# Splitting one weight pair ahead: the order of VectorE's work around the seven-product pairs of a two-layer trunk

## The chip, the cores and the metric

The kernel runs on one core of one Trainium2 chip. The metric is the device time of one execution in microseconds (us). Three executions of the kernel before took 2253.49, 2255.65 and 2257.12 us, median 2255.65 us. A fourth execution was profiled: it took 2254.6 us, and the profile covers 2252.8 us of it.

## The reference

A trunk of two pre-norm residual layers, each a token mixer followed by a SwiGLU feed-forward block (FFN). Layer 0 mixes with HGRN2 and layer 1 with gated linear attention (GLA); both share their input projection with a cross-attention into 256 memory tokens. Sequence 256, model width 2048, FFN width 5632, everything in fp32. Cut to what the change touches:

```python
mem_n = _rmsnorm(mem, norm_mem)
h = x
for layer in range(DEPTH):                      # DEPTH = 2
    hn = _rmsnorm(h, norm_mix[layer])
    if layer % NUM_MIXERS == 0:
        y, xq = _hgrn2_mixer(hn, ...)           # hn @ w_in, then the recurrence
    else:
        y, xq = _gla_mixer(hn, ...)             # the same with q, k, v, g, gk_low, xq
    xa = _memory_attention(xq, mem_n, w_mem_kv[layer])
    h = h + jnp.concatenate([y, xa], axis=-1) @ w_out[layer]
    hn = _rmsnorm(h, norm_ffn[layer])
    gate, up = jnp.split(hn @ w_gate_up[layer], 2, axis=-1)     # 2048 x (2 * 5632)
    h = h + (jax.nn.silu(gate) * up) @ w_down[layer]            # 5632 x 2048
return _rmsnorm(h, norm_final)
```

## The kernel before, in words

**How a product is made.** A product of fp32 matrices is made from halves of each operand: a high part, rounded to the matmul's type, and the low rest. Three matmuls make one product: activations high by weights high, high by low, low by high. The activations' halves are made once per layer; the weights' halves are made as the weights come in.

**How the work is tiled.** Weights arrive as `raw` tiles of 128 partitions by 4 pieces of 512 columns (three buffers). The four pieces are the two row blocks of a *pair* of contraction blocks, crossed with two column blocks c0 and c1. `split` (L276-L303) makes the two halves of a piece or of two pieces: ScalarE writes the high part (a cast) and VectorE subtracts it from the raw piece and writes the low part. The results stand in `parts` tiles (six buffers), or in `part` tiles when only one piece is split (two buffers). The names in the profile carry the number of the raw tile and a letter for the split: `parts128a`, `parts128b`, `parts128c`, `parts128d`. Nearly every instruction is recorded as L151, the wrapper that issues it, so that the tile names tell what an instruction is.

**The kinds of pair.** A 2x2 block product is made plainly with eight products of 128x128 by 512 (24 matmuls), or from seven products of sums and differences (21 matmuls). In the FFN's up part the string `KINDS` gives the kind of each of the eight pairs of an up block: S is a seven-product pair, O a plain one and H a mixed one (both 24 matmuls). All blocks from the fifth on have the plan "SSSSSOSS". There are 11 up blocks of 512 columns per layer, hence seven of these *steady* blocks in each layer, fourteen in all. The pairs of a block are numbered from 0, so that the plain pair is number 5 and the pair ahead of it number 4.

**What a seven-product pair costs VectorE.** `seven` (L451-L466) issues, in this order: the *a* split of raw piece 0; the *b* split of pieces 2 and 3; a subtraction that changes piece 0 (`raw<-raw 128x512`, called *less* here); a subtraction that changes pieces 2 and 3 (`raw<-raw 128x1024`, called *both_less*); the *c* split of pieces 0 and 1; the *d* split of pieces 2 and 3. *less* reads piece 1, to which a second DMA on GpSimd's queue (L444) has added the other row block. *both_less* reads what *less* wrote and writes what *b* reads. *c* reads what *less* wrote, and *d* what *both_less* wrote. A plain pair has two splits of two pieces each; a mixed pair has these, a subtraction, and a split of one piece. In the last pair of a block the summed piece stands in a tile of its own (`T`, `load_apart`), and *c* is split in two instructions.

**What sets the order.** In the FFN each engine executes its instructions in the order of the program (`Engine.kept`). There, TensorE uses the splits of a pair in the order a, b, c, d (products 1, 3, 2, 6, 7, 5, 4; `project_halves`, L627-L668). Between *b* and *less* of each pair a callback `mark` lets work that has come due be issued: copies, gates, transposes and the sums of a finished block (`WHEN`). In the mixer stages a scheduler orders the instructions by its own estimates. The key/query projection of GLA (stages gk0 and gk1, 384 columns, in `gla_pair`) follows a plan in `project_two` (L567-L625) in which "-" is a plain pair.

**The sums.** A finished up block stands in seven PSUM banks. `sums` in `ffn` combines them with seven VectorE additions; two of them release GpSimd to make a low part of the down weights (L300).

## Time and profile before

| what | us |
|---|---|
| median of three executions (lowest, highest) | 2255.65 (2253.49, 2257.12) |
| profiled execution: time, span of its profile | 2254.6, 2252.8 |
| TensorE (PE) busy | 2238.6, 99% of the span |
| VectorE (DVE) busy | 2031.5, 90% |
| ScalarE (ACT) busy | 1452.8, 64% |
| GpSimd (POOL) busy | 280.4, 12% |
| steady blocks of layer 0, 720 to 1168 us: PE busy, DVE busy | 448.0 of 448.0, 426.0 of 448.0 |
| GLA mixer, 1195 to 1480 us: PE busy, DVE busy | 282.4 of 285.0, 224.6 of 285.0 |
| granted TensorE clock | 0.999 of full speed |

A row of the timeline reads: start in us, duration in us, engine, line, operation, tile written, tiles read, shape, how many instructions the row joins, and in brackets the idle time before it and what ended that. The next row of an engine may start before the row ahead of it ends. A row "x2" joins two instructions, and its duration runs from the first one's start to the last one's end. For TensorE the ends are modelled, so that the distance between starts is the safer measure: three matmuls of 512 columns start 0.68 us apart from the next three.

### The profile page before, as it was taken

The page shows a single profiled execution, that of the slowest core. Times are in us where ns is not written, and L with a number is a line of the kernel's source. Part 1 is how long each engine was busy: PE and PEld are TensorE (multiplying, and loading weights), DVE is VectorE, ACT ScalarE, POOL GpSimd, SP SyncE. Part 2 cuts the span into 40 slices and gives each one's busy share as a digit, 9 for nine tenths or more (in the row PEclk, how much of TensorE's full clock was granted, in tenths as well). Part 3 has the DMA queues.
Part 4 walks back from the last instruction along what each step waited for, and adds up shares of the span by engine and source line. Part 5 has one row for each costly group of instructions (what it writes and reads, how often), then busy time and mean ns, then how long its engine had stood idle before and what let it go on. Part 6 is the DMA issues. An engine that isn't in the chain of part 4 may idle for free.

```text
span 2252.8 us, 30400 instructions
## 1 busy us (share of the span) xinstructions
PE 2238.6 (99%) x10668; PEld 1894.6 (84%) x10668; DVE 2031.5 (90%) x2551; ACT 1452.8 (64%) x2010; POOL 280.4 (12%) x275
## 2 busy tenths in 40 slices
PE   9999999999999999999999999999999999999998
PEld 7888888888888888888889999988888888888887
DVE  6879899898998999999996887889999999999997
ACT  7656656565666666666665665566566676666664
POOL 1000100000111112112210000000011221212110
PEclk9999999999999999999999999999999999999999
DMA  8656655656687778878865445566677878887874
GB/s 296 215 168 213 199 182 177 200 193 190 198 236 232 229 234 231 230 230 238 244 221 168 141 156 182 164 209 197 208 221 224 233 230 238 242 238 236 231 233 167
DMA packets 255628, 477.28 MB, mean 212 GB/s; under 512 B 18255, under 2 KB 47731, under 8 KB 255219
## 3 DMA queue, kind: packets, MB, share of 16 engines
q1 hardware_dynamic: 228547, 420.21, 55.5%
q0 software_dynamic: 25632, 50.87, 13.0%
q10 hardware_dynamic: 1296, 4.26, 0.5%
q8 instruction: 84, 1.38, 0.2%
q14 instruction: 69, 0.57, 0.1%
HBM read 472.12 MB, written 3.15 MB: 211 GB/s over the span
## 4 chain that ended last, share of the span: by engine, by line
PE 90%; DVE 6%; issue 2%; DMA 1%; ACT 1%; SPq 0%; POOL 0%; DVEq 0%; POOLq 0%; ACTq 0%
PE f_p L151 34%; PE fd L151 18%; PE wo L151 4%; PE m1p L151 2%; PE hv2p L151 2%; PE hv1p L151 2%; PE hf0p L151 2%; PE hv0p L151 2%; PE wo1p L151 2%; PE hf2p L151 2%; PE hf1p L151 2%; PE wo0p L151 2%; PE m0p L151 2%; PE gk0p L151 1%; PE gk1p L151 1%
## 5 line engine op out<-in xcount | busy, mean ns | idle before, releaser
L151 DVE TENSOR_TENSOR raw<-raw 128x1024 f32<-128x1024 f32 (+3 forms) x330 | 311.2, 943 | 16.7 <-DMA raw<-in_w_down_dram 5.6
L151 ACT CAST parts<-raw 128x1024 fp32r<-128x1024 f32 (+1 forms) x216 | 211.7, 1016 | 56.8 <-DMA raw<-in_w_down_dram 14.7
L151 DVE TENSOR_TENSOR parts<-raw,parts 128x1024 fp32r<-128x1024 f32 (+1 forms) x176 | 200.2, 1171 | 22.7 <-ACT parts L151 22.0
L444 POOL DMA_DIRECT2D raw<-in_w_gate_up_dram x92 | 80.4, 873 | 541.2 <-DMA raw<-in_w_gate_up_dram 274.7
L300 POOL TENSOR_TENSOR parts<-raw,parts 128x1024 fp32r<-128x1024 f32 x40 | 95.6, 2406 | 113.5 <-ACT parts L151 81.2
L151 ACT COPY h<-fd 128x512 f32<-128x512 f32 x80 | 45.7, 588 | 46.5 <-PE fd L151 44.0
L428 POOL DMA_DIRECT2D T<-in_w_gate_up_dram x36 | 21.1, 587 | 430.2 <-DVE hf_4g L151 82.7
L151 ACT ACTIVATE s<-s,rf_r 128x512 f32<-128x512 f32 x44 | 31.8, 723 | 42.0 <-DVE s L151 42.0
L151 DVE SCALAR_TENSOR_TENSOR s<-e,rf_r,s 128x512 f32<-128x512 f32 x44 | 45.7, 1076 | 2.9 <-ACT s L151 0.5
L151 DVE TENSOR_TENSOR e<-f_p,e 128x512 f32<-128x512 f32 x66 | 45.2, 684 | 2.6 <-DVE s L151 0.5
L429 POOL DMA_DIRECT2D T<-in_w_gate_up_dram x36 | 31.0, 861 | 120.4 <-DMA T<-in_w_gate_up_dram 111.1
L151 ACT COPY fd<-h 128x512 f32<-128x512 f32 x82 | 45.2, 582 | 0.0
L444 POOL DMA_DIRECT2D raw<-in_hgrn_w_in_dram x17 | 14.7, 867 | 209.9 <-DMA raw<-in_hgrn_w_in_dram 124.6
L151 PE MATMUL fd<-parts,s_0h 128*128 128x512 f32 x128 | 39.8, 392 | 0.0
L151 PE MATMUL fd<-parts,s_4h 128*128 128x512 f32 x128 | 39.8, 392 | 0.0
L151 PE MATMUL fd<-parts,s_8h 128*128 128x512 f32 x128 | 39.8, 392 | 0.0
L151 PE MATMUL fd<-parts,s_2h 128*128 128x512 f32 x128 | 39.8, 392 | 0.0
L151 PE MATMUL fd<-parts,s_6h 128*128 128x512 f32 x128 | 39.8, 392 | 0.0
L151 PE MATMUL fd<-parts,s_1h 128*128 128x512 f32 x128 | 39.4, 389 | 0.0
L151 PE MATMUL fd<-parts,s_3h 128*128 128x512 f32 x128 | 39.4, 389 | 0.0
L151 PE MATMUL fd<-parts,s_5h 128*128 128x512 f32 x128 | 39.4, 389 | 0.0
L151 PE MATMUL fd<-parts,s_7h 128*128 128x512 f32 x128 | 39.4, 389 | 0.0
(6020 smaller groups left out, 7434.0 us busy)
## 6 DMA issues: line engine op xcount, KB each, us to landing
raw<-in_w_gate_up_dram SPq DMA_DIRECT2D x224, 512.0 KB, 4.4
raw<-in_w_down_dram SPq DMA_DIRECT2D x80, 1024.0 KB, 5.5
raw<-in_w_gate_up_dram SPq DMA_DIRECT2D x220, 256.0 KB, 4.2
raw<-in_hgrn_w_in_dram SPq DMA_DIRECT2D x79, 512.0 KB, 4.6
raw<-in_gla_w_in_dram SPq DMA_DIRECT2D x96, 384.0 KB, 3.3
raw<-in_w_gate_up_dram POOLq DMA_DIRECT2D x92, 256.0 KB, 4.9
T<-in_w_gate_up_dram POOLq DMA_DIRECT2D x72, 256.0 KB, 5.0
raw<-in_w_out_dram SPq DMA_DIRECT2D x16, 1024.0 KB, 5.1
```

The source lines that it names most:

```text
L151: ins = func(*args, **kwargs)
L300: low = (nc.gpsimd if free_port else ve).tensor_tensor(out=both[:, 1, k:j, 0:m], in0=src[:, k:j, :], in1=both[:, 0, k:j, 0:m].bitcast(F32) ...
L428: nc.gpsimd.dma_start(out=both[:, 0, :], in_=rows[0])
L429: nc.gpsimd.dma_start(out=both[:, 0, :], in_=rows[1], accum_op=ALU.add)
L444: nc.gpsimd.dma_start(out=raw[:, 1, 0:n], in_=rows[1], accum_op=ALU.add)
```

## The change

Four edits, none of which changes what is computed.

1. In `project_halves` and `project_two` the raw tile of the next pair is taken, and its *a* split is issued, inside the present seven-product pair between *c* and *d* (argument `ahead`). In `project_two` this is done only where both pairs are seven-product pairs. In a mixed pair the next pair's *a* split is issued ahead of its last split.
2. In a pair that was begun so, *less* is issued ahead of *b*. In a pair with its sum in a tile of its own, *both_less* is issued between the two halves of *c*.
3. `sums` makes its seven additions in another order; the releases stand at the first and the fourth.
4. The plans of gk0 and gk1 become "-----SS-" where they were "------S-": one more seven-product pair in each.

In the FFN the change moves VectorE's instructions as follows. The rows are those of pair 4 and the plain pair 5 of the fifth block of layer 0, on VectorE; `raw_6235` is the raw tile of pair 4 and `raw_6278` that of pair 5. Before:

```order
L151 TENSOR_TENSOR parts128a<-raw_6235,parts128a 128x512
L151 TENSOR_TENSOR parts128b<-raw_6235,parts128b 128x1024
L151 TENSOR_TENSOR raw_6235<-raw_6235 128x512
L151 TENSOR_TENSOR raw_6235<-raw_6235 128x1024
L151 SCALAR_TENSOR_TENSOR parts128c<-raw_6235,parts128c 128x1024
L151 TENSOR_TENSOR parts128d<-raw_6235,parts128d 128x1024
L151 TENSOR_TENSOR parts129a<-raw_6278,parts129a 128x1024
L151 TENSOR_TENSOR parts129b<-raw_6278,parts129b 128x1024
```

The same place with the change, where the tile numbers are `raw_6171` for pair 3, `raw_6211` for pair 4 and `raw_6254` for pair 5:

```order
L151 TENSOR_TENSOR parts128a<-raw_6211,parts128a 128x512
L151 TENSOR_TENSOR parts127d<-raw_6171,parts127d 128x1024
L151 TENSOR_TENSOR raw_6211<-raw_6211 128x512
L151 TENSOR_TENSOR parts128b<-raw_6211,parts128b 128x1024
L151 TENSOR_TENSOR raw_6211<-raw_6211 128x1024
L151 SCALAR_TENSOR_TENSOR parts128c<-raw_6211,parts128c 128x1024
L151 TENSOR_TENSOR parts129a<-raw_6254,parts129a 128x1024
L151 TENSOR_TENSOR parts128d<-raw_6211,parts128d 128x1024
L151 TENSOR_TENSOR parts129b<-raw_6254,parts129b 128x1024
```

Each *a* has moved ahead of the *d* of the pair before, and *less* ahead of *b*. The *a* of a plain pair is two pieces wide (1024 columns), that of a seven-product pair one (512). TensorE's order of use is unchanged in the FFN.

In the GLA stage gk0 the scheduler gives another order too. The rows are VectorE's towards the end of the stage; `gsq` and `gsk` are the sums of the stage's products from PSUM (`gk0p`), `Tg` are decay products, and 232, 233 are raw tiles of the stage that follows. Before:

```order
L151 TENSOR_TENSOR Tg_10701<-GF_10518 128x512
L151 TENSOR_TENSOR Tg_10701<-Tg_10701 128x256
L151 TENSOR_TENSOR parts231b<-raw_10626,parts231b 128x2x384
L151 TENSOR_TENSOR gsq_10637<-gk0p_10605,gsk_10635 128x2x192
L151 TENSOR_TENSOR parts232a<-raw_10676,parts232a 128x2x384
L151 TENSOR_TENSOR gsk_10635<-gk0p_10609,gsq_10637 128x2x192
L151 TENSOR_TENSOR parts232b<-raw_10676,parts232b 128x2x384
L151 TENSOR_TENSOR gsq_10637<-gk0p_10613,gsk_10635 128x2x192
L151 TENSOR_TENSOR gsq_10637<-gk0p_10613,gsq_10637 128x2x192
L151 TENSOR_TENSOR Tg_10701<-Tg_10701 128x128
L151 TENSOR_TENSOR parts233a<-raw_10752,parts233a 128x2x384
L151 TENSOR_TENSOR gsk_10635<-gk0p_10276,gsk_10635 128x2x192
```

With the change:

```order
L151 TENSOR_TENSOR parts231b<-raw_10632,parts231b 128x2x384
L151 TENSOR_TENSOR gsq_10643<-gk0p_10584,gsk_10641 128x2x192
L151 TENSOR_TENSOR parts232a<-raw_10682,parts232a 128x2x384
L151 TENSOR_TENSOR gsk_10641<-gk0p_10588,gsq_10643 128x2x192
L151 TENSOR_TENSOR parts232b<-raw_10682,parts232b 128x2x384
L151 TENSOR_TENSOR gsq_10643<-gk0p_10592,gsk_10641 128x2x192
L151 TENSOR_TENSOR gsq_10643<-gk0p_10592,gsq_10643 128x2x192
L151 TENSOR_TENSOR gsk_10641<-gk0p_10276,gsk_10641 128x2x192
L151 TENSOR_TENSOR gsk_10641<-gk0p_10280,gsk_10641 128x2x192
L151 TENSOR_TENSOR gsq_10643<-gk0p_10288,gsq_10643 128x2x192
L151 TENSOR_TENSOR gsq_10643<-gk0p_10284,gsq_10643 128x2x192
L151 TENSOR_TENSOR Tg_10707<-GF_10518 128x512
```

All sums now stand ahead of the first `Tg`; before, three `Tg` and the split 233a stood ahead of the first of the closing `gsk` sums.

The diff:

```diff
-    def split(src, name, by=2, turned=False):
+    def split(src, name, by=2, turned=False, between=None):
         if isinstance(src, list):
             ...
             for k in (1, 0):
                 ...
+                if k:
+                    between()
...
-    def seven(i, raw, fed, between=None):
+    def seven(i, raw, fed, between=None, b00=None, ahead=None):
         n = raw.shape[2]
         tt = ve.tensor_tensor
-        b00, = split(raw[:, 0:1, :], f"{i}a")
+        apart = fed if fed and fed is not True else None
+        begun = b00 is not None
+
+        def less():
+            tt(out=raw[:, 0, :], in0=apart[:, 0, :] if apart else raw[:, 1, :], in1=raw[:, 0, :], op=ALU.subtract)
+
+        def both_less():
+            tt(out=raw[:, 2:4, :], in0=raw[:, 2:4, :], in1=raw[:, 0:1, :].broadcast_to([P, 2, n]), op=ALU.subtract)
+
+        if not begun:
+            b00, = split(raw[:, 0:1, :], f"{i}a")
+        if not fed:
+            tt(out=raw[:, 1, :], in0=raw[:, 1, :], in1=raw[:, 2, :], op=ALU.add)
+        if fed and begun:
+            less()
         b11, b10 = split(raw[:, 2:4, :], f"{i}b")
         if between:
             between()
-
-        if not fed:
-            tt(out=raw[:, 1, :], in0=raw[:, 1, :], in1=raw[:, 2, :], op=ALU.add)
-        apart = fed if fed and fed is not True else None
-        tt(out=raw[:, 0, :], in0=apart[:, 0, :] if apart else raw[:, 1, :], in1=raw[:, 0, :], op=ALU.subtract)
-        tt(out=raw[:, 2:4, :], in0=raw[:, 2:4, :], in1=raw[:, 0:1, :].broadcast_to([P, 2, n]), op=ALU.subtract)
-        t6, t7 = split([raw[:, 0:1, :], apart] if apart else raw[:, 0:2, :], f"{i}c", turned=True)
+        if not (fed and begun):
+            less()
+        if apart:
+            t6, t7 = split([raw[:, 0:1, :], apart], f"{i}c", turned=True, between=both_less)
+        else:
+            both_less()
+            t6, t7 = split(raw[:, 0:2, :], f"{i}c", turned=True)
+        if ahead:
+            ahead()
         t5, t4 = split(raw[:, 2:4, :], f"{i}d")
...
     # project_two
+        def ahead(at):
+            i, raw = come(at)
+            came.append((i, raw, split(raw[:, 0:1, 0:n], f"{i}a")[0]))
+
+        for at, (p, kind) in enumerate(zip(order, plan)):
+            i, raw, b00 = came.pop() if came else (*come(at), None)
             if kind == "S":
-                todo = held(behind, seven, i, raw[:, :, 0:n], fed) if behind else seven(i, raw[:, :, 0:n], fed)
+                more = (lambda: ahead(at + 1)) if plan[at + 1:at + 2] == "S" else None
+                args = seven, i, raw[:, :, 0:n], fed, None, b00, more
...
     # project_halves
+        def ahead(p):
+            if p < len(PAIRS):
+                i, raw = come(p)
+                came.append((i, raw, split(raw[:, 0:1 if kinds[p] == "S" else 2, :], f"{i}a")))
+
+        for p, kind in enumerate(kinds):
+            Engine.kept = keep <= p
+            i, raw, begun = came.pop() if came else (*come(p), None)
             x = forms[p].get
             last = p == len(PAIRS) - 1
             if kind == "S":
-                todo = seven(i, raw, fed, lambda: mark(key + p))
+                todo = seven(i, raw, apart.get(p, True), lambda: mark(key + p), begun and begun[0], lambda: ahead(p + 1))
                 ...
             else:
-                b00, b01 = split(raw[:, 0:2, :], f"{i}a")
+                b00, b01 = begun or split(raw[:, 0:2, :], f"{i}a")
                 ...
                     ve.tensor_tensor(out=raw[:, 3, :], in0=raw[:, 3, :], in1=raw[:, 2, :], op=ALU.subtract)
+                    ahead(p + 1)
                     e1, = split(raw[:, 3:4, :], f"{i}c")
...
     # gla_pair
-        project_two(hq["pairs"], ("------S-", "------S-")[pr], w, kw + pr * 2 * DK, pr * 2 * DK, 2 * DK, f"gk{pr}", give,
+        project_two(hq["pairs"], "-----SS-", w, kw + pr * 2 * DK, pr * 2 * DK, 2 * DK, f"gk{pr}", give,
...
     # sums, in ffn
-                for out, p, q in ((s0, 2, e0), (e1, 6, e0), (s1, 7, e1), (e1, 5, e1), (e0, 5, s1),
+                for out, p, q in ((e1, 6, e0), (s0, 2, e0), (s1, 7, e1), (e0, 5, s1), (e1, 5, e1),
                                   (s1, 4, s1), (e1, 3, e1)):
                     ve.tensor_tensor(out=out, in0=ps[p], in1=q, op=ALU.add)
-                    if p in (2, 5) and out is not e0 and b:
+                    if (p == 6 or out is e0) and b:
                         free_port.append(ve.last)
```

`come` holds the lines that took a raw tile and loaded it; it is called one pair earlier where `ahead` is.

More of the change, by code (lines that the diff above doesn't have):

```diff
@@ L591, in early, with come @@
                 out[:] = onto
-        for at, (p, kind) in enumerate(zip(order, plan)):
+        came = []
+        def come(at):
             i, raw = new_raw()
             if i == 0:
-                load_pair(raw, w, p, c0, c1, n, kind, fed)
+                load_pair(raw, w, order[at], c0, c1, n, plan[at], fed)
             if prep:
@@ L599, in project_two @@
             if i > 0:
-                load_pair(raw, w, p, c0, c1, n, kind, fed)
+                load_pair(raw, w, order[at], c0, c1, n, plan[at], fed)
+            return i, raw
+        def ahead(at):
[3 more added lines that the diff above has]
+            i, raw, b00 = came.pop() if came else (*come(at), None)
             if kind == "S":
-                todo = held(behind, seven, i, raw[:, :, 0:n], fed) if behind else seven(i, raw[:, :, 0:n], fed)
+                more = (lambda: ahead(at + 1)) if plan[at + 1:at + 2] == "S" else None
+                args = seven, i, raw[:, :, 0:n], fed, None, b00, more
+                todo = held(behind, *args) if behind else args[0](*args[1:])
                 last = at == plan.rindex("S")
@@ L638, in product, with come @@
             pe.matmul(ps[b], xl, hi, start=False, stop=left[b] == 0)
-        for p, kind in enumerate(kinds):
-            Engine.kept = keep <= p
+        came = []
+        def come(p):
             i, raw = new_raw()
@@ L644, in project_halves @@
                 apart[7] = load_apart(w, 7, c1)
-            fed = apart.get(p, True)
-            load_pair(raw, w, p, c0, c1, 512, kind, fed)
+            load_pair(raw, w, p, c0, c1, 512, kinds[p], apart.get(p, True))
+            return i, raw
+        def ahead(p):
[5 more added lines that the diff above has]
+            i, raw, begun = came.pop() if came else (*come(p), None)
             x = forms[p].get
```

## The prediction

> **What bounds the kernel now.** I read the page first: busy shares and the chain of waits (shares by engine), then the windows by stage (busy time of PE, PEld, DVE, ACT and POOL, clock, DMA share).
>
> ```profile
> PE 2238.6 (99%) x10668; PEld 1894.6 (84%) x10668; DVE 2031.5 (90%) x2551; ACT 1452.8 (64%) x2010; POOL 280.4 (12%) x275
> PE 90%; DVE 6%; issue 2%; DMA 1%; ACT 1%; SPq 0%; POOL 0%; DVEq 0%; POOLq 0%; ACTq 0%
> 720.00:1168.00 448.00, 448.00 (x2009) 371.37 (x2008) 426.04 (x464) 301.73 (x385) 83.21 (x76) 1.00 0.79 230
> ```
>
> TensorE bounds the kernel, and in the steady blocks nothing interrupts it. VectorE time saved there is worth nothing by itself; VectorE can only lose, by handing a split over later than TensorE comes to it. So I read who arrives first at each split. VectorE's timeline for the fifth block of layer 0:
>
> ```profile
> 731.50 1.23 DVE L151 SCALAR_TENSOR_TENSOR parts125c<-raw,parts125c 128x1024 fp32r<-128x1024 f32 x1 [0.97 <-ACT parts125c L151]
> 732.64 1.22 DVE L151 TENSOR_TENSOR parts125d<-raw,parts125d 128x1024 fp32r<-128x1024 f32 x1
> 733.78 0.68 DVE L151 TENSOR_TENSOR parts126a<-raw,parts126a 128x512 fp32r<-128x512 f32 x1
> 734.38 1.22 DVE L151 TENSOR_TENSOR parts126b<-raw,parts126b 128x1024 fp32r<-128x1024 f32 x1
> 735.51 1.94 DVE L151 TENSOR_TENSOR raw<-raw 128x512 f32<-128x512 f32 x2
> 737.46 1.23 DVE L151 SCALAR_TENSOR_TENSOR parts126c<-raw,parts126c 128x1024 fp32r<-128x1024 f32 x1
> 738.65 1.23 DVE L151 TENSOR_TENSOR parts126d<-raw,parts126d 128x1024 fp32r<-128x1024 f32 x1
> 739.79 0.68 DVE L151 TENSOR_TENSOR parts127a<-raw,parts127a 128x512 fp32r<-128x512 f32 x1
> ...
> 749.51 1.23 DVE L151 SCALAR_TENSOR_TENSOR parts128c<-raw,parts128c 128x1024 fp32r<-128x1024 f32 x1
> 750.70 1.23 DVE L151 TENSOR_TENSOR parts128d<-raw,parts128d 128x1024 fp32r<-128x1024 f32 x1
> 751.84 1.22 DVE L151 TENSOR_TENSOR parts129a<-raw,parts129a 128x1024 fp32r<-128x1024 f32 x1
> ```
>
> VectorE has no idle time after 731.50. A pair takes it 738.65 − 732.64 = 6.01 us, TensorE's 21 matmuls only 21 × 0.227 = 4.76. So its lead shrinks through the S pairs, and the last splits ahead of plain pair 129 arrive just in time. TensorE's timeline there:
>
> ```profile
> 750.74 0.63 PE L151 MATMUL f_p<-parts128c,hf_4h 128*128 128x512 f32 x2
> ...
> 752.14 0.62 PE L151 MATMUL f_p<-parts128d,hf_4h 128*128 128x512 f32 x2
> 752.60 0.40 PE L151 MATMUL f_p<-parts128d,hf_4l 128*128 128x512 f32 x1
> 752.83 0.62 PE L151 MATMUL f_p<-parts128d,hf_4h 128*128 128x512 f32 x2
> ```
>
> 128c's low part ends at 750.74, when TensorE starts on it; 128d's ends at 751.93, 0.21 before its first matmul. The last steady block of layer 1 shows the same (2164.38 − 2164.17 = 0.21), and the two sets of rows stand for all fourteen:
>
> ```profile
> 2162.94 1.23 DVE L151 TENSOR_TENSOR parts404d<-raw,parts404d 128x1024 fp32r<-128x1024 f32 x1
> 2164.38 0.62 PE L151 MATMUL f_p<-parts404d,hf_4h 128*128 128x512 f32 x2
> ```
>
> **How late is too late.** Three places show it, from VectorE's and TensorE's timelines in blocks 0 and 1:
>
> ```profile
> 534.38 1.22 DVE L151 SCALAR_TENSOR_TENSOR parts87c<-raw,parts87c 128x1024 fp32r<-128x1024 f32 x1
> 535.72 1.22 DVE L151 TENSOR_TENSOR parts87d<-raw,parts87d 128x1024 fp32r<-128x1024 f32 x1
> 582.99 1.22 DVE L151 SCALAR_TENSOR_TENSOR parts96c<-raw,parts96c 128x1024 fp32r<-128x1024 f32 x1
> ```
>
> ```profile
> 535.42 0.73 PE L151 MATMUL f_p<-parts87c,hf_3h 128*128 128x512 f32 x2
> ...
> 536.91 0.63 PE L151 MATMUL f_p<-parts87d,hf_3h 128*128 128x512 f32 x2
> ...
> 583.51 0.40 PE L151 MATMUL f_p<-parts96c,hf_4h 128*128 128x512 f32 x1
> 584.26 0.50 PE L151 MATMUL f_p<-parts96c,hf_4h 128*128 128x512 f32 x1 [0.35 <-DVE parts96c L151]
> 584.60 0.39 PE L151 MATMUL f_p<-parts96c,hf_4l 128*128 128x512 f32 x1
> ```
>
> The first matmul of a split needs only the high part, so the low part may end some 0.17 us after it starts: 87d ends 0.03 after and costs nothing; 87c ends 0.18 after and its two matmuls take 0.73 instead of 0.62; 96c ends 0.70 after, and the next start comes 0.75 instead of 0.23 later (0.52 lost) and the one behind it 0.34 instead of 0.23 (0.11 more). So a stall is lateness less 0.17, plus 0.11 for starting again.
>
> **What pins VectorE.** ScalarE's timeline ahead of 731.50:
>
> ```profile
> 729.24 1.27 ACT L151 COPY h<-fd 128x512 f32<-128x512 f32 x2 [2.31 <-PE fd L151]
> 730.40 1.06 ACT L151 ACTIVATE parts125c<-raw 128x1024 fp32r<-128x1024 f32 x1
> ```
>
> VectorE waits 0.97 for 125c's cast, which stands behind copies that wait for TensorE. The copies come due behind *b* of pair 1 before and after the change, so *c* of pair 1 stays at 731.50 on TensorE's clock, and whatever is saved ahead of it is lost in this wait.
>
> **Part 1 and 2, steady blocks.** From the rows: an instruction of two pieces starts its successor after 1.14 when the successor doesn't need it (732.64 to 733.78), one of one piece after 0.60 (733.78 to 734.38). Where each needs the one before, *less* and *both_less* take 1.95 (735.51 to 737.46) instead of 0.60 + 1.14 = 1.74, and *c* to *d* takes 1.19 instead of 1.14; the dependences cost 0.26 per pair. In the new order *both_less* still stands right behind *b*, whose source it overwrites: one wait remains, which I put at about 0.12, half of the 0.21 lost around *both_less*. So the pair comes to 1.14 + 0.60 + 1.14 + 0.60 + 1.14 + 0.12 + 1.14 = 5.88, and from the pinned *c* of pair 1 to *c* of pair 4 it takes 17.64 instead of 749.51 − 731.50 = 18.01. So 128c starts at 749.14, 0.37 earlier, for which TensorE isn't waiting.
>
> Then comes the cost. Between 128c and 128d stands 129a now, and this is of two pieces: 1.14. So 128d starts at 749.14 + 1.14 + 1.14 = 751.42 and ends at 752.65, 0.51 after TensorE's 752.14. Less 0.17 that is 0.34 of stall, and 0.11 to start again: **0.45 per steady block, 6.3 for fourteen**. If the remaining wait were nothing, 128d would end 0.36 earlier, 0.15 after TensorE's start, and the stall would vanish (0 in all); if nothing were saved, 128d would end at 753.06, stall 0.76 + 0.11, 12.2 in all. I stay near the rows. 129a loses nothing, since TensorE reaches it at the end of 128d. In the S pairs that follow VectorE has 3.2 us in hand (plain pair: 2 × 1.14 = 2.28 against 24 × 0.227 = 5.44), so their later *d* and earlier *c* cost and gain nothing.
>
> **Blocks 0 to 3.** In the mixed pairs the next *a* fills the gap ahead of the last split (0.69 idle at such a place), but 96d then takes the delay that 96c loses: about even, from −0.6 to +0.6 per layer. 87d ends 0.03 after its matmul now and gets 88a ahead of it (1.14), of which earlier gains give back perhaps 0.8: +0.3. 106d, ahead of plain pair 107, has 0.37 in hand:
>
> ```profile
> 636.52 1.23 DVE L151 TENSOR_TENSOR parts106d<-raw,parts106d 128x1024 fp32r<-128x1024 f32 x1
> 638.12 0.62 PE L151 MATMUL f_p<-parts106d,hf_4h 128*128 128x512 f32 x2
> 624.87 0.86 POOL L444 DMA_DIRECT2D raw<-in_w_gate_up_dram  x1 [5.58 <-DVE parts104c L151]
> ```
>
> It loses 1.14 and gains perhaps 0.5: +0.2. But *less* now wants the adding DMA that GpSimd issues at 624.87 about 2 us sooner (1.14 for *b*, the rest from the filled gaps), and *b*, which needs none of it, queues behind: up to +0.4 more. Together +0.6 per layer, **+1.2**.
>
> **Part 3** saves two dependences per block, off the path: VectorE has its lead then, and is pinned afterwards. Nothing; were it exposed, 0.2 × 22 = 4 at most.
>
> **Part 4.** Each stage drops three matmuls of 384 columns; twelve start 1245.93 − 1243.85 = 2.08 apart, 0.173 each. That is 0.52 a stage, **−1.0**. VectorE gets about 2.6 us more work, ScalarE 1.2, estimated from the pieces; TensorE leads there are over 0.9 us. The sums move ahead of the decays, so TensorE's wait for ScalarE's scaled keys shrinks:
>
> ```profile
> 1243.85 2.24 PE L151 MATMUL gk0p<-parts226a,hm_3x 128*128 128x384 f32 x12
> 1245.93 1.03 PE L151 MATMUL ap<-ident,prob 128*128 128x128 f32 x8
> ...
> 1278.31 0.44 PE L151 MATMUL tgk<-ident,gsk 128*128 128x128 f32 x2 [0.59 <-ACT gsk L151]
> 1279.56 0.44 PE L151 MATMUL tgk<-ident,gsk 128*128 128x128 f32 x2 [0.80 <-ACT gsk L151]
> ```
>
> Of 1.4, I take **−0.6**; the ends are −1.4 and, if the added work makes a split late, +2.
>
> **Sum** against the profiled execution's 2254.6: +6.3 + 1.2 − 1.0 − 0.6 = +5.9, thus 2260.5. The profiled execution lies 1.0 under the median, and on its scale I predict **2261**.
>
> **A rule against the saving.** The rows above overlap (733.78 starts before 732.64 + 1.22) where there is no dependence, and don't at 737.46. The Trainium skill ("VectorE: DVE Perf Modes", section "The DRAIN you can't avoid") says that the next operation doesn't start before the pipe is empty and that "the semaphore costs nothing extra here"; the same section allows an earlier start to an operation that isn't held. By the first rule reordering would save VectorE nothing; the trace, with 1.95 against 1.74, disagrees.
>
> **Rivals.** (a) *The delay of 128d is covered*: VectorE gains more per pair than I count, or a late low part is tolerated longer. For it: the remaining wait is not in this trace. Against: 96c's stall begins by the same rule. It decides if 128d ends before 752.31, which asks 0.34 more gain over three pairs than the 0.37 counted: nearly the whole of the remaining wait. Then parts 3 and 4 and recovered stalls remain: −1.0 − 0.6 − 1.2, about 2253: not slower. Chance 0.22.
> (b) *The order saves nothing*: what an instruction takes doesn't depend on its neighbour, and 128d is late by all of 1.14 − 0.21 − 0.17, plus 0.11: 14 × 0.87 + 1.2 − 1.6 = +11.8, 2267. For it: *c* to *d* takes 1.19 though they don't depend on each other directly; against: 1.95 against 1.74. Chance 0.08. It is what the skill's rule above would make of this change.
> (c) *`less` at the head of the queue waits for DMA* in steady blocks too: VectorE stands, with *b* and all behind it. From a landing 0.3 us after *less* is wanted, 128d is 0.3 later still: 14 × 0.3 = 4.2 more, 2265. For it: the adding DMA is asked for earlier in every S pair; against: DMA share 0.79, with landings some 5 us after issue. Chance 0.10.
>
> **How the numbers follow.** My forecast has the remaining 0.60, itself spread from 2257 to 2264. Slower by over 0.2% (4.5 us, about what a measurement of this kernel can tell from no change) begins at 2260.2: 0.6 of the forecast, and (b) and (c): 0.54. Faster, under 2251.1, needs (a) with more than its sum: 0.09. The rest, 0.37, is no change. Eight times in ten: 2252.5 to 2266.
>
> **What would show it.** Right: TensorE's second start on 128d's successors in each steady block late by 0.2 to 0.5, put down to VectorE, with 129a just ahead of it; VectorE's pair period near 5.9; *c* of pair 1 still waiting on ScalarE; gk stages 0.5 shorter. Wrong: no wait of TensorE in steady blocks (a); a period of 6.0 (b); VectorE idle ahead of `raw<-raw` for a DMA (c).

## The result

The changed kernel is slower: 2270.39 us in the median of six executions (2269.58 to 2272.92) beside 2254.80 of the kernel before in the same rounds (2252.85 to 2257.12). The ratio is 1.0070, with a 95% interval of 1.0057 to 1.0083: 15.6 us more. The prediction of 2261 had the sign, and its range ended at 2266.

The page of the changed kernel, busy shares and chain of waits by engine:

```profile
PE 2246.2 (99%) x10662; PEld 1892.7 (83%) x10662; DVE 2027.7 (89%) x2561; ACT 1453.7 (64%) x2014; POOL 283.2 (12%) x275
PE 73%; DVE 14%; issue 8%; DMA 2%; ACT 2%; SPq 0%; POOL 0%; ACTq 0%; DVEq 0%; POOLq 0%
```

VectorE does about as much work as before, but its share of the chain that sets the end has gone from 6 to 14%, and TensorE's from 90 to 73%: the chain now leaves TensorE where it waits for a split.

Where the time went is seen best by setting the two traces beside each other at the same place of TensorE's program. In this table the time is that of the first matmul on the split named, after minus before (in the last row the end of the span); the last column is what was added since the row above.

| first matmul on | what lies since the row above | shift, us | added, us |
|---|---|---|---|
| 87d | start, HGRN mixer, up to pair 3 of block 0 | +0.81 | +0.81 |
| 88a | d of pair 3 of block 0 | +1.45 | +0.64 |
| 97a | block 1 | +1.53 | +0.08 |
| 107a | block 2 | +2.83 | +1.30 |
| 117a | block 3 | +4.13 | +1.30 |
| 201a | the seven steady blocks of layer 0 | +7.08 | +2.95 |
| 210d | the down tail of layer 0 | +8.59 | +1.51 |
| 291d | GLA mixer, output projection | +7.47 | −1.12 |
| 292a | block 0 of layer 1 | +8.11 | +0.64 |
| 301a | block 1 | +10.16 | +2.05 |
| 311a | block 2 | +11.24 | +1.08 |
| 321a | block 3 | +12.54 | +1.30 |
| 405a | the seven steady blocks of layer 1 | +15.57 | +3.03 |
| end | the rest | +15.77 | +0.20 |

The fourteen steady blocks add 6.0 and blocks 0 to 3 of both layers 8.4, where 6.3 and 1.2 had been forecast. A steady block of the change, VectorE's timeline and then TensorE's:

```profile
735.64 1.23 DVE L151 SCALAR_TENSOR_TENSOR parts125c<-raw,parts125c 128x1024 fp32r<-128x1024 f32 x1 [1.21 <-ACT parts125c L151]
...
747.39 1.22 DVE L151 SCALAR_TENSOR_TENSOR parts127c<-raw,parts127c 128x1024 fp32r<-128x1024 f32 x1
748.53 0.68 DVE L151 TENSOR_TENSOR parts128a<-raw,parts128a 128x512 fp32r<-128x512 f32 x1
749.13 1.22 DVE L151 TENSOR_TENSOR parts127d<-raw,parts127d 128x1024 fp32r<-128x1024 f32 x1
750.26 0.69 DVE L151 TENSOR_TENSOR raw<-raw 128x512 f32<-128x512 f32 x1
750.87 1.22 DVE L151 TENSOR_TENSOR parts128b<-raw,parts128b 128x1024 fp32r<-128x1024 f32 x1
752.12 1.23 DVE L151 TENSOR_TENSOR raw<-raw 128x1024 f32<-128x1024 f32 x1
753.26 1.22 DVE L151 SCALAR_TENSOR_TENSOR parts128c<-raw,parts128c 128x1024 fp32r<-128x1024 f32 x1
754.39 1.22 DVE L151 TENSOR_TENSOR parts129a<-raw,parts129a 128x1024 fp32r<-128x1024 f32 x1
755.53 1.22 DVE L151 TENSOR_TENSOR parts128d<-raw,parts128d 128x1024 fp32r<-128x1024 f32 x1
```

```profile
756.25 0.39 PE L151 MATMUL f_p<-parts128d,hf_4h 128*128 128x512 f32 x1
756.80 0.50 PE L151 MATMUL f_p<-parts128d,hf_4h 128*128 128x512 f32 x1 [0.17 <-DVE parts128d L151]
757.14 0.40 PE L151 MATMUL f_p<-parts128d,hf_4l 128*128 128x512 f32 x1
```

Pair 1's *c* still waits for ScalarE. A pair now takes VectorE 753.26 − 747.39 = 5.87 us. But 129a stands between 128c and 128d, and 128d ends at 756.75, 0.50 after its first matmul. The next start comes 0.55 later instead of 0.23, and the one behind it 0.34 instead of 0.23. All fourteen blocks show it, with 0.33 of stall in thirteen and 0.61 in one, each with the 0.11 behind it.

In blocks 1 to 3 the same stall is larger and something stands ahead of it. Block 3 of layer 0, VectorE, ScalarE, TensorE:

```profile
682.71 1.22 DVE L151 SCALAR_TENSOR_TENSOR parts115c<-raw,parts115c 128x1024 fp32r<-128x1024 f32 x1
685.61 0.69 DVE L151 TENSOR_TENSOR parts116a<-raw,parts116a 128x512 fp32r<-128x512 f32 x1 [1.68 <-ACT parts116a L151]
686.56 1.23 DVE L151 TENSOR_TENSOR parts115d<-raw,parts115d 128x1024 fp32r<-128x1024 f32 x1 [0.26 <-ACT parts115d L151]
```

```profile
684.95 0.62 ACT L151 CAST parts116a<-raw 128x512 fp32r<-128x512 f32 x1 [3.33 <-PE f_p L151]
685.48 1.05 ACT L151 CAST parts115d<-raw 128x1024 fp32r<-128x1024 f32 x1
```

```profile
693.26 0.39 PE L151 MATMUL f_p<-parts116d,hf_4h 128*128 128x512 f32 x1
694.24 0.50 PE L151 MATMUL f_p<-parts116d,hf_4h 128*128 128x512 f32 x1 [0.60 <-DVE parts116d L151]
```

ScalarE can't cast 116a until TensorE has gone on, and now 115d's cast, which used to stand ahead of it, stands behind it. VectorE waits 1.68 us. 116d used to be ready 0.88 us ahead of its first matmul; now it ends 0.93 behind it (694.19 against 693.26).

Two waits for a DMA stand ahead of *less* with *b* behind them; VectorE in the down tail of layer 0 and in block 1 of layer 1, then TensorE in the tail:

```profile
1165.88 0.69 DVE L151 TENSOR_TENSOR raw<-raw 128x512 f32<-128x512 f32 x1 [5.44 <-DMA raw<-in_w_down_dram]
...
1632.28 0.69 DVE L151 TENSOR_TENSOR raw<-raw 128x512 f32<-128x512 f32 x1 [1.48 <-DMA raw<-in_w_gate_up_dram]
```

```profile
1179.59 1.45 PE L151 MATMUL fd_0p<-parts210c,s_20m 128*128 128x512 f32 x5 [1.30 <-DVE parts210c L151]
```

In the order of before, the tail's wait was 4.01 us long and *b* stood ahead of it; now *b* stands behind.

The down tail of layer 1 has the same order. VectorE there, with the change:

```profile
2216.33 0.69 DVE L151 TENSOR_TENSOR raw<-raw 128x512 f32<-128x512 f32 x1 [4.53 <-DMA raw<-in_w_down_dram]
2216.94 1.22 DVE L151 TENSOR_TENSOR parts413b<-raw,parts413b 128x1024 fp32r<-128x1024 f32 x1
```

Before, 413b stood ahead of the wait, and the wait was 1.60 us. TensorE loses 0.2 at most by it in this execution, but more in several of the runs below.

### The profile page after: what moved, and what is told of

Same layout as the page of the kernel before. It is cut to its first block, busy times and chain, and to the rows that moved or that the text cites. A ratio compares the mean times of both kernels' runs of the same rounds, so it can differ in the third digit from the quotient of the medians.

```text
span 2268.6 us, 30382 instructions
## 1 busy us (share of the span) xinstructions
PE 2246.2 (99%) x10662; PEld 1892.7 (83%) x10662; DVE 2027.7 (89%) x2561; ACT 1453.7 (64%) x2014; POOL 283.2 (12%) x275
## 4 chain that ended last, share of the span: by engine, by line
PE 73%; DVE 14%; issue 8%; DMA 2%; ACT 2%; SPq 0%; POOL 0%; ACTq 0%; DVEq 0%; POOLq 0%
PE f_p L151 19%; PE fd L151 16%; PE wo L151 4%; DVE raw L151 2%; PE m1p L151 2%; PE hv2p L151 2%; PE hv1p L151 2%; PE hv0p L151 2%; PE hf0p L151 2%; PE wo1p L151 2%; PE hf2p L151 2%; PE hf1p L151 2%; PE wo0p L151 2%; PE m0p L151 2%; DMA raw<-in_w_gate_up_dram 2%
## 5 line engine op out<-in xcount | busy, mean ns | idle before, releaser
L151 ACT CAST parts<-raw 128x1024 fp32r<-128x1024 f32 (+1 forms) x216 | 211.7, 1016 | 57.9 <-DMA raw<-in_w_down_dram 15.6
L151 DVE SCALAR_TENSOR_TENSOR s<-e,rf_r,s 128x512 f32<-128x512 f32 x44 | 54.8, 1284 | 2.5
```

The lines of the kernel that those rows point to most:

```text
L151: ins = func(*args, **kwargs)
```

## The experiments

Three theories, each with its place. **T1**: a split of two pieces ahead of *d* makes *d* late (steady blocks, 87d, 291d, and part of blocks 1 to 3). **T2**: a one-piece split taken ahead waits for one of its two buffers, with *d* behind it (blocks 1 to 3). **T3**: *less*, ahead of *b*, waits for its DMA. The rivals of each theory are the other two, or a cause that none of them names. The kernel before was run beside each set: 2255.82 (25 executions) for the first four runs, 2255.03 (19) for the next four, 2255.72 (26) for the last three.

**1. The two-piece split behind d.**

```diff
-        if ahead:
+        if ahead and not late:                 # late: the next pair is plain or mixed
             ahead()
         t5, t4 = split(raw[:, 2:4, :], f"{i}d")
+        if ahead and late:
+            ahead()
```

> The changed kernel with one thing undone: where the next pair is plain or mixed, its two-piece a split is issued behind the d split of the present seven-product pair again, instead of ahead of it. Theory T1 (the wide split ahead of d makes d late): the 14 stalls of 0.45 us at the d of pair 4 of the steady blocks vanish (-6.4), those at 87d and 291d too (-1.3), and the stalls of 0.9 at the d ahead of the plain pair in blocks 1 to 3 (six places, -5.3): about 13 us less than the change, 2 to 3 us over the kernel before. Rival T2 (blocks 1 to 3 lose their time because the a split of pair 4 waits for a buffer): the six places keep most of their 1.25 us each, and the run comes out some 7 to 8 us under the change, 7 to 8 over the kernel before.

2257.04 us (10 executions), ratio to before 1.0007, interval 0.9998 to 1.0017. The fourteen stalls are gone, as are those at 87d and 291d and at the six places of blocks 1 to 3; the whole loss but about 1 us came with this one split's place. VectorE and TensorE in the same block:

```profile
750.84 1.23 DVE L151 TENSOR_TENSOR parts128d<-raw,parts128d 128x1024 fp32r<-128x1024 f32 x1
751.98 1.22 DVE L151 TENSOR_TENSOR parts129a<-raw,parts129a 128x1024 fp32r<-128x1024 f32 x1
```

```profile
752.54 0.61 PE L151 MATMUL f_p<-parts128d,hf_4h 128*128 128x512 f32 x2
```

128d ends 0.47 ahead of its matmul, where before it was 0.21: the 0.26 that reordering saves VectorE by then is real, and TensorE doesn't get it. What stayed were short stalls at 106c, 116c and 320c (0.37, 0.39, 0.39), which T1 doesn't explain, 1.2 in the down tail of layer 0 and 0.8 at 414c in that of layer 1.

With the two-piece split out of the way, the run also shows what the rest of the new order does ahead of plain pair 107. VectorE and TensorE at 106d:

```profile
636.81 1.23 DVE L151 TENSOR_TENSOR parts106d<-raw,parts106d 128x1024 fp32r<-128x1024 f32 x1
```

```profile
638.14 0.61 PE L151 MATMUL f_p<-parts106d,hf_4h 128*128 128x512 f32 x2
```

106d ends only 0.1 ahead of its first matmul, where it was 0.37 before; 116d and 320d are at 0.13 where they were at 0.88.

**2. The buffer's turn.**

```diff
                     ve.tensor_tensor(out=raw[:, 3, :], in0=raw[:, 3, :], in1=raw[:, 2, :], op=ALU.subtract)
+                    mine = single(f"{i}c")     # the one-piece buffer, taken before the next pair's
                     ahead(p + 1)
-                    e1, = split(raw[:, 3:4, :], f"{i}c")
+                    e1, = split(raw[:, 3:4, :], f"{i}c", both=mine)
```

> The changed kernel with one thing undone: in a mixed pair the buffer of its own last split (one piece, one of two buffers) is taken ahead of that of the next pair's a split, as it was before; the order of the instructions stays that of the change. T2: the a split of pair 4 in blocks 1 to 3 (96a, 106a, 116a and the same in layer 1) waits for the buffer of the mixed pair's split, which TensorE has left by then, and no longer for that of the pair just ahead; VectorE no longer stands 1.7 us at 116a; the six places lose 1.25 us each now and 0 to 0.5 then: 4 to 6 us less than the change. T1 alone: the steady blocks keep 0.45 each, and if the wide split is what makes the six places late, they keep 0.9 each: 1.5 to 2.5 us less than the change.

2270.75 us (4 executions), ratio 1.0064, interval 1.0047 to 1.0081: nothing gained. T2 in this form fell. ScalarE waits as long as in the change; its row of this run, and then that of the kernel before:

```profile
686.18 0.62 ACT L151 CAST parts116a<-raw 128x512 fp32r<-128x512 f32 x1 [3.32 <-PE f_p L151]
```

```profile
682.10 0.62 ACT L151 CAST parts116a<-raw 128x512 fp32r<-128x512 f32 x1 [0.84 <-PE f_p L151]
```

With TensorE's shift at the first matmul on 115a or 116c taken off (4.09 here, 2.86 in the change), the cast begins at 682.09 in both, and at 682.10 in the kernel before. The wait was there before too, and which buffer is taken first doesn't move the moment at which it ends.

**3. Both.**

> The changed kernel with both: the wide a split behind d, and the mixed pair's buffer taken first. T1 and T2 together: no stall at any d or c of pair 4; what is left is the stall of 1.5 us in the down tail of layer 0 and whatever less, ahead of b, waits for its DMA (1.5 us of VectorE's time at 300b), against 1 us gained in the two key/query stages: within 2 us of the kernel before, 13 to 15 us under the change. If a third cause of several us is at work, it stays 4 us or more above the kernel before.

2258.57 us (10 executions), ratio 1.0007, interval 0.9998 to 1.0017: the same as the first run within the interval. So the second edit adds nothing to the first either, and no further cause of several us is left. The profiled execution has the stalls of the first run, with 1.75 and 0.9 in the two tails, and one of 0.7 at 404c.

**4. Less behind b as well.**

```diff
-        if fed and begun:
-            less()
         b11, b10 = split(raw[:, 2:4, :], f"{i}b")
...
-        if not (fed and begun):
-            less()
+        less()
```

> As the run with both undone, and in addition less stands behind b again in every begun pair, also in the mixer and tail stages (what remains is one a split ahead of d where both pairs are seven-product pairs, the split c of the last pair, the sums and the key/query plans). T3 (less ahead of b waits for its adding DMA, with b queued behind): the stall of 1.5 us in the down tail goes, as does VectorE's wait ahead of 300b: 1.5 to 2.5 us under the run with both undone. Rival (the dependences it removed were worth something): VectorE's pair grows from 5.87 to some 6.0 us, 128d ends 0.3 later than with both undone, still ahead of TensorE by 0.3: no difference, or up to 2 us more.

2258.61 us (10 executions), ratio 1.0016, interval 1.0006 to 1.0025; the one without is within it. In the trace TensorE's wait at 210c, 1.6 with both undone, is gone, but the edit isn't the reason: *b* still stands behind the wait. 209 is not begun ahead, as a plain pair stands in front of it, so every version of the program has its *b* ahead of *less*; it is the scheduler that turned the two round in the tail. VectorE:

```profile
1159.96 0.69 DVE L151 TENSOR_TENSOR raw<-raw 128x512 f32<-128x512 f32 x1 [3.23 <-DMA raw<-in_w_down_dram]
1160.57 1.22 DVE L151 TENSOR_TENSOR parts209b<-raw,parts209b 128x1024 fp32r<-128x1024 f32 x1
```

The data came earlier this time: with TensorE's shift at 208a taken off, *less* began at 1157.46, against 1159.06 with both undone. So this run doesn't test T3 in the tail, and neither do runs 8 and 9, whose tails have this order as well. Which part of the change made the scheduler choose it, no run shows.

What speaks for T3 there is the set of traces, on the same scale. With *b* behind, 210c stalls by 0.7 to 1.8 us in the four in which *less* began at 1157.9 or later (the change, runs 1, 3 and 5), and at most 0.2 is lost in the five in which it began by 1157.5 (runs 2, 4, 6, 8, 9); run 7 has another order there. With *b* ahead it doesn't stall even at 1158.95 (before) and 1158.76 (run 11). So the order costs up to 1.8 us there when the DMA is late, and nothing when it is early. In the tail of layer 1 the edit leaves the order too, and TensorE loses 0.5 at 414c.

In the FFN, where the edit does take effect, the time didn't get better: against run 3 the steady blocks of layer 0 add about 1 us, in steps of 0.1 to 0.25.

**5. Mixed pairs not ahead.**

```diff
                     ve.tensor_tensor(out=raw[:, 3, :], in0=raw[:, 3, :], in1=raw[:, 2, :], op=ALU.subtract)
-                    ahead(p + 1)
                     e1, = split(raw[:, 3:4, :], f"{i}c")
```

> The changed kernel with one thing undone: a mixed pair no longer splits the next pair's a ahead of its own last split (seven-product pairs still do, two pieces ahead of d included). In the run with the buffer taken first the wait only moved: there 105a, issued ahead of the mixed pair's split 104c, waited for TensorE to leave 103c's buffer. T2, mended (with two buffers and a split more in flight, one of 104c, 105a, 106a waits for TensorE with others behind it): now order and turns are those of before, VectorE no longer stands 2.3 us at 104c or 1.7 at 116a, and of the 7.1 us that blocks 1 to 3 lose in both layers about 2.7 remain (96d 0.8, 106d 0.56, 116d 0, in each layer, by the two-piece split alone): 4 to 5 us under the change, some 11 over the kernel before. Rival (the two-piece split alone makes these places late): 0 to 1 us under the change.

2274.49 us (4 executions), ratio 1.0087, interval 1.0072 to 1.0102: 4 us *worse* than the change, against an expected gain of 4 to 5. Both the expectation and its rival (a gain of 0 to 1) missed. Taking the next split ahead in a mixed pair fills a gap and is a gain: without it block 0 loses 1.09 instead of 0.64, and 95c and 299c stall too. And 116a still waits for TensorE, with 115d behind it:

```profile
687.19 0.62 ACT L151 CAST parts116a<-raw 128x512 fp32r<-128x512 f32 x1 [1.40 <-PE f_p L151]
687.71 1.05 ACT L151 CAST parts115d<-raw 128x1024 fp32r<-128x1024 f32 x1
```

The wait is shorter because ScalarE comes to it later, not because it ends sooner (687.19 − 5.09 of shift = 682.10). So the moment is TensorE's, and what can be chosen is only what stands behind the wait.

**6. Half a dose.** The two-piece split of a plain or mixed pair in two instructions, one ahead of *d*, one behind.

```diff
+                if kinds[p] != "S" and apiece:
+                    halves, piece = by_piece(raw[:, 0:2, :], f"{i}a")
+                    came.append((i, raw, halves))
+                    piece(0)
+                    return lambda: piece(1)    # called behind d
```

> The changed kernel with a dose: the a split of a plain or mixed pair is made piece by piece, the first piece ahead of d and the second behind it. By the rule of the prediction 128d ends 0.54 earlier than in the change, at 752.11 on the time scale of before, 0.03 ahead of its first matmul: no stall in the steady blocks (-6.4), and -0.5 at each of the eight other places: 2259 to 2261. Rival (any split between c and d breaks the handing over, whatever its length): the steady blocks keep their 0.45, 2270.

2260.28 us (10 executions), ratio 1.0023, interval 1.0014 to 1.0032. The steady blocks have no stall. VectorE, TensorE:

```profile
752.99 0.68 DVE L151 TENSOR_TENSOR parts129a<-raw,parts129a 128x512 fp32r<-128x512 f32 x1
753.60 1.22 DVE L151 TENSOR_TENSOR parts128d<-raw,parts128d 128x1024 fp32r<-128x1024 f32 x1
```

```profile
754.85 0.62 PE L151 MATMUL f_p<-parts128d,hf_4h 128*128 128x512 f32 x2
```

128d ends at 754.82, 0.03 ahead, the number expected. What is left over before lies in blocks 1 to 3 (0.2 to 0.4 at each *c* and *d* of pair 4), in the tail of layer 1 (1.1 at 414c), and in parts that the change doesn't touch.

**7. A double dose.** The plain pair's *b* ahead of *d* too.

```diff
                 came.append((i, raw, split(raw[:, 0:1 if kinds[p] == "S" else 2, :], f"{i}a")))
+                if kinds[p] == "O" and kinds[p - 1] == "S":
+                    later_b.append(split(raw[:, 2:4, :], f"{i}b"))
```

> The changed kernel with a double dose: where a plain pair follows, its b split (two pieces) stands ahead of d as well. By the rule 128d ends 1.14 later than in the change: the stall grows from 0.33 + 0.11 to 1.47 + 0.11 in each of the fourteen steady blocks (+16), and by 1.14 at eight other places (those two ahead of a mixed pair keep theirs) (+9): 2294 to 2297. Rival (VectorE has slack that the pin hides): less than half of it, under 2283.

2294.11 us (4 executions), ratio 1.0174, interval 1.0157 to 1.0191: inside the range expected. TensorE:

```profile
759.70 0.39 PE L151 MATMUL f_p<-parts128d,hf_4h 128*128 128x512 f32 x1
761.39 0.50 PE L151 MATMUL f_p<-parts128d,hf_4h 128*128 128x512 f32 x1 [1.30 <-DVE parts128d L151]
761.73 0.40 PE L151 MATMUL f_p<-parts128d,hf_4l 128*128 128x512 f32 x1
```

1.69 instead of 0.23 (1.46 lost) and 0.34 instead of 0.23: 1.57 per steady block, expected 1.58. The 1.14 more of VectorE's work ahead of 128d cost 1.13 more of TensorE's time. So once what is in hand is used up (0.47 in run 1, and the 0.17 that cost nothing), the lateness of 128d passes on one for one.

**8. A version drawn from these.** A split ahead only between two seven-product pairs, *less* behind *b* in `project_two`; no new diff.

> A version drawn from these: a split ahead of d only between two seven-product pairs of the FFN, mixed pairs as before, a plain pair's a behind d, less behind b again in project_two (mixer and tails), the sums and both key/query plans of the change. All three theories: no stall is added; 0.4 to 0.5 us saved in each key/query stage: 2254 to 2256 beside 2255.8 before, too little to be told from it. If the tail of layer 0 still stalls by 1.5 us, less was not its cause and the run is 1 us above the kernel before.

2258.29 us (10 executions), ratio 1.0015, interval 1.0006 to 1.0025: 3 us over before, which wasn't expected. Its profiled execution has the key/query stages' gain and no stall of 1.5 in the tail (0.2 there), but one of 1.33 at 383c in a steady block, where VectorE waited 1.5 for ScalarE's cast of 383a, 0.37 and 0.39 at 106c and 116c again, and 0.8 at 414c. 383a was late because ScalarE had waited for the DMA of its raw tile:

```profile
2049.42 0.62 ACT L151 CAST parts383a<-raw 128x512 fp32r<-128x512 f32 x1 [2.12 <-DMA raw<-in_w_gate_up_dram]
```

382d's cast stood behind it: a split taken ahead waits for its data with *d* behind it, as it waits for its buffer in T2. What made that DMA late isn't known.

**9. No split ahead behind a mixed pair.** As 1, with *less* behind *b* in `project_two`, and

```diff
-                todo = seven(..., lambda: ahead(p + 1), ...)
+                todo = seven(..., None if p and kinds[p - 1:p + 2] == "HSS" else lambda: ahead(p + 1), ...)
```

> The run with the wide a behind d, and in addition the a split is not taken ahead in a seven-product pair that stands behind a mixed pair (pair 3 of blocks 1 to 3); less stands behind b in project_two. T2, as the traces of the first runs leave it: with two buffers for one-piece splits, 106a and 116a can't be made before TensorE has left the buffer's last owner, and taken ahead they hold 105d and 115d behind them (ScalarE waited 2.4 and 3.2 us there). Behind d, as before, the wait holds nothing: the three short stalls of 0.37 to 0.39 at 106c, 116c and 320c, which every run so far has kept, vanish. With 0.4 saved in each key/query stage and the stalls at 96c and 300c gone (0.64 and 0.41): 0.5 to 2 us under the kernel before. Rival (these stalls come from the sums or the other edits): 0.37 at 106c and 0.39 at 116c stay.

2257.09 us (11 executions), ratio 1.0006, interval 0.9997 to 1.0015. ScalarE and TensorE, first of run 1 and then of this one:

```profile
629.86 0.62 ACT L151 CAST parts106a<-raw 128x512 fp32r<-128x512 f32 x1 [2.40 <-PE f_p L151]
630.39 1.05 ACT L151 CAST parts105d<-raw 128x1024 fp32r<-128x1024 f32 x1
...
636.42 0.96 PE L151 MATMUL f_p<-parts106c,hf_4h 128*128 128x512 f32 x2
```

```profile
628.78 1.05 ACT L151 CAST parts105d<-raw 128x1024 fp32r<-128x1024 f32 x1 [1.33 <-DVE raw L151]
629.85 0.62 ACT L151 CAST parts106a<-raw 128x512 fp32r<-128x512 f32 x1
...
636.40 0.62 PE L151 MATMUL f_p<-parts106c,hf_4h 128*128 128x512 f32 x2
```

106a is cast at the same time in both; with 105d ahead of it 106c is in time. The stalls at 106c and 320c are gone, which shows T2 in its last form. 106d gains as well:

```profile
635.81 1.23 DVE L151 TENSOR_TENSOR parts106d<-raw,parts106d 128x1024 fp32r<-128x1024 f32 x1
```

```profile
637.76 0.62 PE L151 MATMUL f_p<-parts106d,hf_4h 128*128 128x512 f32 x2
```

It ends 0.72 ahead of its matmul, where run 1 has 0.1 and the kernel before 0.37. At 116c there is a stall of 0.97, for another reason: *less* of 116 waited 1.65 for an adding DMA that GpSimd had issued at 677.34. The stall at 414c (0.7) is there too.

```profile
677.34 0.86 POOL L446 DMA_DIRECT2D raw<-in_w_gate_up_dram  x1 [6.77 <-DVE raw L151]
...
686.22 1.95 DVE L151 TENSOR_TENSOR raw<-raw 128x512 f32<-128x512 f32 x2 [1.65 <-DMA raw<-in_w_gate_up_dram]
```

**10. The key/query plans alone.** The kernel before with "-----SS-" in both stages.

> The kernel before with the two key/query plans of the change and nothing else. The prediction: -0.52 a stage for three matmuls of 384 columns and -0.6 in all for a shorter wait for the scaled keys: 1.6 us less. As the trace of the change has it: some 0.4 a stage, 0.8 less. Either is hardly to be told from no change in the times; the profile's places behind the two stages decide.

2256.86 us (11 executions), ratio 1.0000, interval 0.9991 to 1.0009. On TensorE's timeline the shift goes from −0.39 at the first matmul of gk0 to −1.09 behind gk1: 0.7 us gained, too little for the times. In the change it goes from 8.42 to 7.62, 0.8. TensorE's waits for the scaled keys:

```profile
1277.54 0.44 PE L151 MATMUL tgk<-ident,gsk 128*128 128x128 f32 x2 [0.27 <-ACT gsk L151]
1278.78 0.87 PE L151 MATMUL tgk<-ident,gsk 128*128 128x128 f32 x6 [0.81 <-ACT gsk L151]
```

1.4 became 1.1. From its first matmul to its last, gk1 is 0.5 shorter, and gk0 0.2 here and 0.4 in the change.

**11. The sums alone.**

```diff
-                for out, p, q in ((s0, 2, e0), (e1, 6, e0), (s1, 7, e1), (e1, 5, e1), (e0, 5, s1),
+                for out, p, q in ((e1, 6, e0), (s0, 2, e0), (s1, 7, e1), (e0, 5, s1), (e1, 5, e1),
```

> The kernel before with the new order of the sums and nothing else. The prediction: nothing, since VectorE has its lead there and is pinned behind it: within 0.3 us of the kernel before on TensorE's clock. Rival (an earlier release of GpSimd's splits or of the banks shows): more than 0.5 us either way; and if the short stalls at 106c and 116c belong to the sums, they show here.

2254.80 us (11 executions), ratio 0.9995, interval 0.9986 to 1.0004. No stall at 106c or 116c; the steady blocks don't move. In the times it is nothing, as forecast. In the trace the two short stalls of the kernel before, at 96c and 300c, are gone (0.5 and 0.3 us), as they mostly are in the versions with the split ahead; run 10, with the old sums, has them at 0.4 and 0.7. Whether the sums did it isn't shown.

None of these versions beats the kernel before by more than its interval.

## Why the prediction was right about the sign and wrong about the size

**Right, by its own steps.** TensorE bounds the steady blocks, and VectorE can only lose: runs 1, 6 and 7 show it. The pin at *c* of pair 1 held (1.21 us of waiting for ScalarE). The pair of 5.88 us measured 5.87, and the remaining wait, put at 0.12, measured 752.12 − 750.87 = 1.25 instead of 1.14. 128d was to end 0.51 after its first matmul and ended 0.50 after it; the stall was to be 0.34 + 0.11 and was 0.33 + 0.11. The fourteen blocks were to add 6.3 and added 6.0. The sums were worth nothing (run 11).

By the Trainium skill's page "VectorE: DVE Perf Modes", section "The DRAIN you can't avoid", order and waits between VectorE's instructions would change nothing. The pair's 6.01 before and 5.87 after disagree with that and agree with the same section's exception for an operation that isn't held. Rival (b) fell with it.

**Wrong: blocks 0 to 3.** The step that failed is "It loses 1.14 and gains perhaps 0.5", said of 106d. It assumed that what VectorE saves ahead of such a place is kept. Behind a mixed pair it isn't: a one-piece split taken ahead stands in front of 105d and 115d and can't be made before TensorE has moved on, so VectorE's gain turns into a wait of up to 1.68 us. In place of a gain of 0.5 the runs show a loss. With the two-piece split out of the way (run 1), 106d ends 0.1 ahead of its matmul instead of 0.37; with the one-piece split out of the way too (run 9), 0.72. In the change it ends 0.95 late, so that the two-piece split is worth some 1.06. Taken from run 9's 0.72 that would leave 106d 0.34 late, which by the prediction's own rule costs 0.28, near its +0.2: what it missed there was this wait. The prediction also left out 116d and 320d, which were 0.88 early in the kernel before; run 1 has them at 0.13, and run 9 has 320d at 0.88 again.

The term was 1.2; it measured 8.4. Of its places, the *d* with a two-piece split ahead of it cost 0.89 to 0.92 in blocks 2 and 3 and *c* another 0.16 to 0.39; run 1 takes the first away, and run 9 the second at 106c and 320c. At 87d and 291d 0.64 was lost each instead of 0.3: by run 1 the earlier gains give back 0.67 there, near the 0.8, but with 88a ahead of it 87d ends 1.34 later and not 1.14. Block 1 of layer 1 alone added 2.05, with VectorE's 1.48 of waiting for the DMA just ahead of it; how much of it belongs to which wasn't separated.

**Half right: rival (c).** It was given 0.10 and placed in the steady blocks, where VectorE waited for such a DMA only twice, 0.2 and 1.1 us; the 0.61 at 344d is another matter, since there VectorE waited longer at the pin (1.49 us at 341c). It came with more weight in block 1 of layer 1 and in the down tails, a part of the program that the prediction never looked at and put at nothing: 1.5 us in that of layer 0 in this execution. In other runs with the same tail the loss was between 0 and 1.8, and at 414c, in the tail of layer 1, 0.5 to 1.1 in runs 1, 3, 4, 6, 8 and 9. This tail is part of why none of them gets under the kernel before.

**Mis-sized: the key/query stages.** −1.6 was forecast and −0.7 to −0.8 measured (run 10 and the change). The matmuls gave 0.7 to 0.9 of the 1.0; of the 0.6 for the scaled keys 0.3 came, and later waits gave most of that back.

**Not foreseen, and not to be put down to the change**: 0.8 us up to pair 3 of block 0. The shift is +1.0 at 8a already, and runs 10 and 11, whose code up to there is that of the kernel before, have −0.3 and +1.6 at 8a and +1.5 and +3.0 at 87a.

Added up, 6.0 + 8.4 + 1.5 − 1.1 + 0.8 + 0.2 = 15.8, the table's shift. These are terms of one execution against one, and the stretch up to 87a shows that one of them can be off by a microsecond or more. What remains open is why the DMAs of the raw tiles take so much longer in some executions, and what made the scheduler turn *b* and *less* round in the tails.

## What to carry to other kernels

When the engine that bounds the kernel is fed in order, look for the instruction with the least time in hand and ask first what the new order puts ahead of *it*: run 7's dose shows that its lateness passes to TensorE one for one, while time saved ahead of a wait that another engine ends passes on nothing. An instruction that is taken ahead brings its own waits along, for its buffer and its data, and everything that used to stand ahead of it now stands behind them; its moment is often set by another engine and doesn't come sooner. And the parts of a program that a shared function touches in passing (here the tail and the mixed pairs) want the same reading as the one that the edit was made for.

## What the runs showed of the hardware that I had not expected

The adding DMA of one pair, of 256 KB, was issued at 677.34 in run 9 and landed at 685.78, 8.4 us later. In the kernel before the same DMA took 4.1 (675.10 to 679.18), and the median of such DMAs on its page is 4.9. GpSimd also issued it 2.6 us later on TensorE's timeline; no run shows what slowed it after that. And the 0.11 that TensorE loses on the matmul behind a stall is the same whatever the stall was: it was 0.34 instead of 0.23 after the 0.52 at 96c before the change, after the 0.33 of the steady blocks and after the 1.46 of run 7.
